# Sums over a head's 64 channels moved from TensorE products with ones to VectorE turns and GpSimd copies, in a FoX and RWKV-7 layer

## The chip, the cores and the metric

The kernel runs on one NeuronCore of a Trainium2 chip. The metric is device microseconds from start to end of one execution, as the median of several runs; lower is better.

## What is computed

The layer takes `x` of 256 frames by 4096 channels, all in float32. One projection `x @ w_in` gives the columns of 16 heads of forgetting attention (128 wide), of 32 heads of RWKV-7 time mixing (64 wide) and of a gate. The RWKV-7 part needs three sums over the 64 channels of a head, for each frame. In the reference they are:

```python
kk = (kr * k_k).reshape(hs)
kk = kk / jnp.maximum(jnp.linalg.norm(kk, axis=-1, keepdims=True), 1e-12)
...
y = _rwkv7_scan(rh, decay.reshape(hs), kh, vh, -kk, kk * ah)
mu = jnp.mean(y, axis=-1, keepdims=True)
var = jnp.mean(jnp.square(y - mu), axis=-1, keepdims=True)
y = ((y - mu) * lax.rsqrt(var + GN_EPS)).reshape(B, S, RWKV_WIDTH) * gn_gain + gn_bias
bonus = jnp.sum(rh * kh * r_k, axis=-1, keepdims=True) * vh
```

These are the squared norm of the key, the bonus sum of `r * k * r_k`, and the variance of the readout. Both head groups are then gated, multiplied by `w_out` (4096 x 4096), added to the scaled input and normalised.

## The kernel before

**The weight stream.** TensorE multiplies float32 data as two rounded halves: `split` (line 137) makes from a loaded tile `w` (128 x 1024) its high half `w_Nh` by ScalarE (line 140) and the low half `w_Nl` by VectorE (line 141). A product is then three matmuls of 128 x 512: x high by w high (line 146), x low by w high (147), x high by w low (148). A tile makes 12 such matmuls. The main loop goes over 8 pairs `n` of 128-channel groups, four blocks `b` per pair (r and k; v; two blocks of attention and gate columns) and 16 tiles a block; then the output projection (`project`, lines 849 to 854) goes over 8 column blocks in the same way. There are three buffers for low halves and four for high halves and for raw tiles.

**What runs beside it.** Everything else is written as Python generators (`ahead`, which runs `prepare` for the 16 groups, `chain`, which runs `rwkv` for the 8 pairs, `fox`, `unload`). The loop calls `slot()` after every two groups of three matmuls, and each call moves every generator on by one `yield`; `wait(W[...])` counts such slots. A scheduler below then sets the order on each engine's queue, and each queue runs in order. So VectorE's queue holds the weight splits with the pieces of all generators between them.

**`prepare(i)`, lines 451 to 503** (16 times). Two rows of 256 frames are made in `sb`: the squared key (ScalarE, line 470) and `r * r_k * k` (VectorE, 471). For their sums over the 64 partitions of a head, `sb` is split into halves `sh` (ScalarE, 475) and `sl` (VectorE, 476), and two matmuls with a 128 x 128 block matrix of ones (`onesr`, made at line 187 from the constants at 72 and 73) put the sums, already on all 64 partitions, into PSUM tile `nps` (490, 491). VectorE takes the maximum of the norm with 1e-24 (493) and its reciprocal over 256 columns (496); ScalarE copies the bonus sum into `bon` (494). The reciprocal goes into `ae` (498) and `BK` (501).

**`rwkv(n)`, lines 505 to 703** (8 times). After the chunked recurrence, the readout of a pair lies in PSUM tile `yp`. ScalarE squares it into `sd` (683) and copies it scaled (685); the squares are split (688, 689), two matmuls with `onesr` sum them into `vs` (692, 693), ScalarE takes the root of the 512 columns (694), and VectorE two reciprocals of 256 columns (696), two products (698) and two sums (699), ahead of the gate (`gate`, 371).

**GpSimd** is used for masks of the attention (`affine_select`, line 713, on a tile that SyncE's queue loads), for the token shift of v (521 to 523), for a product (519) and for zeroing `eL` (438) and `SV` (605); its queue runs in order too. The tile `shl` has one buffer, which is also used for `yr` and for `BKt` (546).

Of the kernel before, what the change touches and what calls it, by code (L numbers as in the profile page):

```python
# [10 lines left out]
F32 = mybir.dt.float32  # L11
BF16 = mybir.dt.bfloat16
F32R = mybir.dt.float32r
AF = mybir.ActivationFunctionType
ALU = mybir.AluOpType
AX = mybir.AxisListType

P = 128
S = 256
# [5 lines left out]
HD = 64  # L25
# [25 lines left out]
B = 32  # L51
# [1 line left out]
NJ = B // NG  # L53
C_ID = 0
C_MASK = 128
C_ONES = 256
C_E = 384
C_SCAN = 640
C_ROW = C_SCAN + S
C_W = C_ROW + 2  # L60
LW = 2 * LORA + NF


def constants():
    p = np.arange(P)[:, None]
    s = p % C
    t = np.arange(C)[None, :]
    cst = np.zeros((P, C_W), np.float32)
    cst[:, C_ID : C_ID + P] = np.eye(P)
    cst[:, C_MASK : C_MASK + C] = s < t  # L70
    cst[:, C_MASK + C : C_MASK + 2 * C] = s <= t
    same = (np.arange(P)[:, None] // HD) == (np.arange(P)[None, :] // HD)
    cst[:, C_ONES : C_ONES + P] = same
    j = (p % NG) * NJ + np.arange(P)[None, :] // B
    cst[:, C_E : C_E + P] = j == np.arange(P)[None, :] % B
    cst[:, C_SCAN : C_SCAN + S] = (np.arange(S)[None, :] % C) != 0
    first = np.array([1, 1, 0, 1, 0, 1], np.float32)
    sign = np.array([-1, -1, -1, 1, 1, 1], np.float32)
    cst[:6, C_ROW] = sign * (2 * first - 1)
    cst[:6, C_ROW + 1] = sign * (1 - first)  # L80
    return cst
# [3 lines left out]
def layer(ctx: ExitStack, tc: tile.TileContext, xt, xtok, w_lora, w_main, muv, w_o, up, par, mulora, fbias, lng, lnb, cst, out):  # L85
    nc = tc.nc
    PS = bass.MemoryType.PSUM

    const = ctx.enter_context(tc.tile_pool(name="const", bufs=1))
# [5 lines left out]
    def pst(name):  # L95
        return ps.tile([P, 512], F32, tag="ps", name=name)

    cs = const.tile([P, C_W], F32, name="cs")
# [14 lines left out]
    for n, (k0, k1) in enumerate(pieces):  # L113
        raw = spool.tile([P, 2 * S], F32, tag="xr", name=f"xr{n}", bufs=4)
        nc.sync.dma_start(out=raw[:, : (k1 - k0) * S], in_=xt[:, k0:k1, :].rearrange("p k t -> p (k t)"))
        x_raw.append(raw)
        raw = spool.tile([P, 2 * LW], F32, tag="lr", name=f"lr{n}", bufs=4)
        (nc.scalar if n < 3 else nc.sync).dma_start(out=raw[:, : (k1 - k0) * LW], in_=w_lora[:, k0:k1, :].rearrange("p k c -> p (k c)"))
        l_raw.append(raw)
# [9 lines left out]
    nc.sync.dma_start(out=cs, in_=cst)  # L129

    ident = cs[:, C_ID : C_ID + P]
    ones = cs[:, C_ONES : C_ONES + P]

    def column(name, i):
        return prm[:, PAR.index(name), i : i + 1]
# [21 lines left out]
    for n, (k0, k1) in enumerate(pieces):  # L157
        for k in range(k0, k1):
            t = xpool.tile([P, 2, S], F32R, tag=f"x{k}", name=f"x{k}")
            r = x_raw[n][:, (k - k0) * S : (k - k0 + 1) * S]  # L160
            tc.keep_in_program_order(nc.scalar.copy(t[:, 0, :], r))
            nc.vector.tensor_tensor(t[:, 1, :], r, t[:, 0, :].bitcast(F32), ALU.subtract)
            xs.append(t)
        hi, lo = split(l_raw[n], (k1 - k0) * LW, f"wl{n}", spool, str(n % 3), 2 * LW)
        for j, m in steps(k1 - k0, False):
            mm(acc_l[m], m, k0 + j, hi, lo, j * LW, LW)
        hi, lo = split(w_raw[n], (k1 - k0) * OB, f"wr{n}")
# [15 lines left out]
    nc.vector.tensor_scalar(hka[:, 1, :], prm[:, ika, :], -0.5, 1.0, ALU.mult, ALU.add)  # L183
    gneps = const.tile([P, 1], F32, name="gneps")
    nc.vector.memset(gneps, GN_EPS)
    onesr = const.tile([P, P], F32R, name="onesr")
    nc.vector.tensor_copy(onesr, ones)

    sides = []

# [70 lines left out]
    rp = mid.enter_context(tc.tile_pool(name="rp", bufs=1))  # L261
# [9 lines left out]
    def rt(name):  # L271
        return t256("t", name, 5)
# [122 lines left out]
    def flat(t):  # L395
        return t.rearrange("p a b -> p (a b)")
# [18 lines left out]
    def front(i):  # L415
# [19 lines left out]
        L = rt(f"L{i}")  # L435
        nc.vector.tensor_tensor_scan(L, cs[:, C_SCAN : C_SCAN + S], tw, 0.0, ALU.mult, ALU.add)
        eL = rp.tile([P, NCH, C + 1], F32, tag="eL", name=f"eL{i}")
# [10 lines left out]

    KB = [(slice(0, C), slice(C, P)), (slice(C, P), slice(0, C))]

    def prepare(i):
        n, u = divmod(i, 2)
        while u == 0 and n and n - 1 not in done:
            yield
        eL, eI, am, ae = yield from front(i)
        while (i, 1) not in rk:
            yield
        r, kr = rk[i, 0], rk[i, 1]
        if u == 0:
            pairs[n] = dict(  # L460
                lc=rp.tile([P, 2, NCH], F32, tag="lc", name=f"lc{n}"),
                BK=rp.tile([P, 2, NCH, P], F32, tag="BK", name=f"BK{n}"),
                lt=[rp.tile([P, 2, NCH, P], F32, tag=f"lt{j}", name=f"lt{j}_{n}") for j in range(2)],
                bon=rp.tile([P, 2, S], F32, tag="bon", name=f"bon{n}"),
            )
        q = pairs[n]
        k = rt(f"k{i}")
        nc.vector.tensor_tensor(k, kr, am, ALU.mult)
        sb = rp.tile([P, 2, S], F32, tag="Nb", name=f"sb{i}")
        nc.scalar.activation(sb[:, 0, :], kr, AF.Square, scale=column("k_k", i))  # L470
        nc.vector.scalar_tensor_tensor(sb[:, 1, :], r, column("r_k", i), k, ALU.mult, ALU.mult)
        yield
        shl = rp.tile([P, 2, 2, S], F32R, tag="shl", name=f"shl{i}")
        sh, sl = flat(shl[:, 0]), flat(shl[:, 1])
        nc.scalar.copy(sh, flat(sb))
        nc.vector.tensor_tensor(sl, flat(sb), sh.bitcast(F32), ALU.subtract)
        yield
        BK = q["BK"][:, u]
        lt = [q["lt"][j][:, u] for j in range(2)]
        nc.scalar.copy(q["lc"][:, u, :], eL[:, :, C])  # L480
        nc.vector.scalar_tensor_tensor(lt[0][:, :, 0:C], ch(kr), nkk[:, i : i + 1], eL[:, :, 0:C], ALU.mult, ALU.mult)
        nc.vector.tensor_tensor(lt[0][:, :, C:P], ch(r), eL[:, :, 1:], ALU.mult)
        nc.scalar.copy(lt[1][HALF[1]], lt[0][HALF[1]])
        yield
        for j in range(2):
            h = HALF[j]
            nc.vector.tensor_tensor(BK[h, :, KB[j][1]], ch(k)[h], ch(eI)[h], ALU.mult)
        yield from wait(W["np"] if n else 2 * W["np"])
        nps = pst(f"np{i}")
        nc.tensor.matmul(nps, onesr, sl, start=True, stop=False)  # L490
        nc.tensor.matmul(nps, onesr, sh, start=False, stop=True)
        n2 = rt(f"n2{i}")
        nc.vector.tensor_scalar(n2, nps[:, :S], 1e-24, None, ALU.max)
        nc.scalar.copy(q["bon"][:, u, :], nps[:, S:])
        yield
        tc.keep_in_program_order(nc.vector.reciprocal(n2, n2))
        yield from wait(2)
        nc.vector.scalar_tensor_tensor(ae, ae, 0.5, n2, ALU.mult, ALU.mult)
        for j in range(2):
            h = HALF[j]  # L500
            nc.vector.scalar_tensor_tensor(BK[h, :, KB[j][0]], ch(kr)[h], column("k_k", i)[h], ch(ae)[h], ALU.mult, ALU.mult)
        yield
        prepared.add(i)

    def rwkv(n):
# [3 lines left out]
        q = pairs[n]  # L509
        lc, BK, lt, bon = q["lc"], q["BK"], q["lt"], q["bon"]  # L510
# [9 lines left out]
        p, t = bks[n], vs_[n]  # L520
# [10 lines left out]
        for u in range(2):  # L531
# [3 lines left out]
            for a in range(4):  # L535
                o = B * (a % 2)
                nc.sync.dma_start(out=nd[u, a].rearrange("c r s -> r c s"), in_=gb[a // 2][B * a : B * (a + 1), u, :, o : o + B])
            nc.sync.dma_start(out=flat(nb[:, u]), in_=nd[u].rearrange("q c r s -> (q c) (r s)").unsqueeze(1).to_broadcast([16, NG, B * B]))
        for u in range(2):
            for j in range(2):  # L540
                o = HALF[1 - j]
# [30 lines left out]
        xc = rp.tile([P, 2, NJ, B], F32, tag="xc", name=f"xc{n}")  # L572
        ev = cs[:, C_E : C_E + P].rearrange("p (j s) -> p j s", s=B)
        for u in range(2):
# [21 lines left out]
        for j in range(2):  # L596
            o = HALF[1 - j]
# [9 lines left out]
        for a in range(4):  # L607
            o = C * (a // 2) + B * (a % 2)
# [3 lines left out]
        for u in range(2):  # L612
            for c in range(NCH):
                for j in range(2):
                    a, b = slice(C * j, C * j + B), slice(C * j + B, C * j + C)
# [17 lines left out]
        for u in range(2):  # L633
            for c in range(NCH):
                for j in range(2):
                    a, b = slice(C * j, C * j + B), slice(C * j + B, C * j + C)
                    nc.tensor.matmul(xp[a, u * P + c * B : u * P + (c + 1) * B], Q[b, u, c, :], X[b, u, c, C * j + B : C * j + C], start=True, stop=True)
        for j in range(2):
            a = slice(C * j, C * j + B)
# [7 lines left out]
        for c in range(NCH):  # L647
# [10 lines left out]
            if c < NCH - 1:  # L658
# [11 lines left out]
                if 0 < c + 1 < NCH - 1:  # L670
                    sl = rp.tile([P, 2, C], F32, tag="sl", name=f"sl{n}_{c}")
# [10 lines left out]
        yc, sd = post[:, 0:2], post[:, 2:4]  # L682
        nc.scalar.activation(flat(sd), yp, AF.Square)
        for u in range(2):
            nc.scalar.mul(yc[:, u], yp[:, u * S : (u + 1) * S], column("gn_gain", i0 + u))
        yr = rp.tile([P, 2, 2, S], F32R, tag="shl", name=f"yr{n}")
        yh, yl = flat(yr[:, 0]), flat(yr[:, 1])
        nc.scalar.copy(yh, flat(sd))
        nc.vector.tensor_tensor(yl, flat(sd), yh.bitcast(F32), ALU.subtract)
        yield from wait(W["vs"])  # L690
        vs = pst(f"vs{n}")
        nc.tensor.matmul(vs, onesr, yl, start=True, stop=False)
        nc.tensor.matmul(vs, onesr, yh, start=False, stop=True)
        nc.scalar.activation(flat(sd), vs, AF.Sqrt, scale=1.0 / HD, bias=gneps)
        for u in range(2):
            nc.vector.reciprocal(sd[:, u], sd[:, u])
            yield
            nc.vector.tensor_tensor(yc[:, u], yc[:, u], sd[:, u], ALU.mult)
            nc.vector.tensor_tensor(yc[:, u], yc[:, u], bon[:, u], ALU.add)
            while f"r{i0 + u}" not in szs or 2 * (i0 + u) + 1 >= FAR and not closed:  # L700
                yield
            yield from gate(yc[:, u], f"r{i0 + u}", 2 * (i0 + u) + 1)
# [208 lines left out]
    for b, q in outs:  # L911
        if q == 0:
            pool, tag = (ps, "ps") if b == 1 or b and b % 2 == 0 else (pp, "pp")
# [115 lines left out]
    for n in range(HALVED):  # L1029
        b = HALVED + n  # L1030
        finish(1, b, l1, pp, "pp")
        o = slice(n * OB, (n + 1) * OB)
# [52 lines left out]
```

## Time and profile before

| What | Value |
|---|---|
| Median of 3 runs | 1958.2 us (1957.36 to 1959.06) |
| Profiled execution, first to last instruction (span) | 1956.1 us |
| Profiled execution, time outside the span | not listed; the median run is 2.1 us above the span |
| TensorE busy | 1937.4 us, 99% of the span |
| VectorE busy | 1368.3 us, 70% |
| ScalarE busy | 981.2 us, 50% |
| GpSimd busy | 81.2 us, 4% |

Busy time is the time in which an engine has an instruction in work. Matmuls overlap one another: their records last longer than the distance from one to the next, and the cost of one is read from that distance. The page writes PE for TensorE, DVE for VectorE, ACT for ScalarE, POOL for GpSimd and SP for SyncE. L141 is line 141 of the kernel, and a name such as `w_7l` is the tile that the instruction writes.

### The profile page before, as it was taken

The numbers are of one execution on the slowest core, as the hardware profiler recorded it, in microseconds if no ns is written. First come the engines' busy times: TensorE is split into PE (matmuls) and PEld (weight loads), VectorE is DVE, ScalarE is ACT, GpSimd is POOL, SyncE is SP. The second block draws the span as 40 slices with busy tenths as digits, with TensorE's granted clock in tenths as the row PEclk, the third lists the DMA queues.
The fourth block names the chain that finished last, engine by engine and source line by source line (L and its number), as shares of the span: only waits on it lengthen the run. The fifth ranks groups of instructions, "written<-read, shape, count | busy, mean of one in ns | idle before, by whom it ended". The sixth has DMA issues, their size and how long they took to land.

```text
span 1956.1 us, 28202 instructions
## 1 busy us (share of the span) xinstructions
PE 1937.4 (99%) x10169; PEld 1586.9 (81%) x10169; DVE 1368.3 (70%) x2212; ACT 981.2 (50%) x1485; POOL 81.2 (4%) x111
## 2 busy tenths in 40 slices
PE   9998999999999999999999999999999999999998
PEld 7887778888887888788878887888788878888886
DVE  6587667866886688667857785778577856755555
ACT  6553555455545554565456545644564454433332
POOL 0010001000100010001000100010001000000000
PEclk9999999999999999999999999999999999999999
DMA  9577657867686778676867686778677777766564
GB/s 337 145 237 198 206 163 244 226 194 213 212 233 186 215 215 232 192 220 208 232 185 225 208 236 183 225 209 234 178 231 211 241 274 236 255 199 199 189 198 168
DMA packets 269392, 420.13 MB, mean 215 GB/s; under 512 B 142338, under 2 KB 171028, under 8 KB 269252
## 3 DMA queue, kind: packets, MB, share of 16 engines
q1 hardware_dynamic: 268820, 417.91, 70.7%
q8 instruction: 80, 1.31, 0.3%
q10 hardware_dynamic: 432, 0.43, 0.1%
q14 instruction: 60, 0.49, 0.1%
HBM read 388.61 MB, written 29.64 MB: 214 GB/s over the span
## 4 chain that ended last, share of the span: by engine, by line
PE 86%; DMA 1%; DVE 0%; ACT 0%; issue 0%; DVEq 0%; ACTq 0%; SPq 0%
PE acc L146 21%; PE acc L148 20%; PE acc L147 20%; PE oacc L852 6%; PE oacc L854 6%; PE oacc L853 6%; PE yp L678 1%; PE gp L517 1%; PE up L653 1%; PE rh L626 1%; PE sp L662 0%; DMA wo<-in_w_o_dram 0%; PE fsp L717 0%; PE fop L736 0%; PE tp L550 0%; DMA h<-hd 0%
## 5 line engine op out<-in xcount | busy, mean ns | idle before, releaser
L582 DVE TENSOR_REDUCE xc<-prod 128x8 f32<-128x16 f32 (+30 forms) x248 | 73.2, 295 | 6.7
L579 DVE TENSOR_TENSOR prod<-Nb,xc 128x8 f32<-128x8 f32 (+30 forms) x248 | 71.6, 289 | 6.6
L141 DVE TENSOR_TENSOR w_10l<-w,w_10h 128x1024 fp32r<-128x1024 f32 x31 | 37.9, 1223 | 37.8 <-PE acc L148 21.6
L141 DVE TENSOR_TENSOR w_6l<-w,w_6h 128x1024 fp32r<-128x1024 f32 x31 | 38.9, 1256 | 34.9 <-ACT w_6h L140 18.6
L141 DVE TENSOR_TENSOR w_8l<-w,w_8h 128x1024 fp32r<-128x1024 f32 x31 | 37.8, 1219 | 32.9 <-ACT UV L656 13.6
L141 DVE TENSOR_TENSOR w_0l<-w,w_0h 128x1024 fp32r<-128x1024 f32 x31 | 37.9, 1222 | 31.3 <-ACT w_0h L140 14.8
L141 DVE TENSOR_TENSOR w_5l<-w,w_5h 128x1024 fp32r<-128x1024 f32 x31 | 38.3, 1235 | 29.3 <-PE acc L148 17.4
L148 PE MATMUL acc<-w_7l,x 128*128 128x512 f32 x124 | 49.5, 399 | 5.4 <-DVE w_7l L141 5.4
L141 DVE TENSOR_TENSOR w_7l<-w,w_7h 128x1024 fp32r<-128x1024 f32 x31 | 37.9, 1222 | 22.3 <-PE acc L148 13.2
L141 DVE TENSOR_TENSOR w_11l<-w,w_11h 128x1024 fp32r<-128x1024 f32 x31 | 37.9, 1222 | 21.0 <-PE acc L148 13.5
L141 DVE TENSOR_TENSOR w_12l<-w,w_12h 128x1024 fp32r<-128x1024 f32 x31 | 37.5, 1211 | 20.6 <-PE acc L148 16.1
L141 DVE TENSOR_TENSOR w_14l<-w,w_14h 128x1024 fp32r<-128x1024 f32 x31 | 38.0, 1227 | 19.9 <-issue 11.1
L140 ACT CAST w_0h<-w 128x1024 fp32r<-128x1024 f32 x31 | 32.7, 1053 | 38.3 <-PE acc L147 21.7
L140 ACT CAST w_5h<-w 128x1024 fp32r<-128x1024 f32 x31 | 32.6, 1053 | 37.9 <-PE acc L147 37.9
L140 ACT CAST w_8h<-w 128x1024 fp32r<-128x1024 f32 x31 | 32.6, 1050 | 37.7 <-DMA w<-in_w_main_dram 31.3
L146 PE MATMUL acc<-w_7h,x 128*128 128x512 f32 x124 | 51.0, 411 | 0.0
L140 ACT CAST w_13h<-w 128x1024 fp32r<-128x1024 f32 x31 | 32.5, 1049 | 36.4 <-PE acc L147 22.9
L146 PE MATMUL acc<-w_5h,x 128*128 128x512 f32 x124 | 50.5, 408 | 0.0
L146 PE MATMUL acc<-w_8h,x 128*128 128x512 f32 x124 | 50.0, 404 | 0.4 <-ACT w_8h L140 0.4
L140 ACT CAST w_9h<-w 128x1024 fp32r<-128x1024 f32 x31 | 32.4, 1046 | 35.6 <-PE acc L147 32.9
L146 PE MATMUL acc<-w_3h,x 128*128 128x512 f32 x124 | 50.2, 405 | 0.0
L140 ACT CAST w_7h<-w 128x1024 fp32r<-128x1024 f32 x31 | 32.6, 1052 | 34.9 <-PE acc L147 19.7
(813 smaller groups left out, 6549.3 us busy)
## 6 DMA issues: line engine op xcount, KB each, us to landing
w<-in_w_main_dram SPq DMA_DIRECT2D x496, 512.0 KB, 3.9
wo<-in_w_o_dram SPq DMA_DIRECT2D x128, 512.0 KB, 3.8
bt<-bk SPq DMA_DIRECT2D x88, 128.0 KB, 4.0
Nb<-nd SPq DMA_DIRECT2D x16, 512.0 KB, 5.0
wr<-in_w_main_dram SPq DMA_DIRECT2D x15, 512.0 KB, 7.1
hd<-hl SPq DMA_DIRECT2D x29, 256.0 KB, 4.4
h<-hd SPq DMA_DIRECT2D x29, 256.0 KB, 6.1
raw<-bt SPq DMA_DIRECT2D x16, 256.0 KB
```

The costliest lines, as they stand in the source:

```text
L140: nc.scalar.copy(hi[:, :n], src[:, :n])
L141: nc.vector.tensor_tensor(lo[:, :n], src[:, :n], hi[:, :n].bitcast(F32), ALU.subtract)
L146: nc.tensor.matmul(acc[:, :n], xs[k][:, 0, tt], hi[:, o : o + n], start=(k == 0), stop=False)
L147: nc.tensor.matmul(acc[:, :n], xs[k][:, 1, tt], hi[:, o : o + n], start=False, stop=False)
L148: nc.tensor.matmul(acc[:, :n], xs[k][:, 0, tt], lo[:, o : o + n], start=False, stop=(k == KT - 1))
L517: nc.tensor.matmul(gp[u][j][:, c * P : (c + 1) * P], BK[h, u, c, :], lt[j][h, u, c, :], start=True, stop=True)
L579: first = nc.vector.tensor_tensor(prod[:, :, :, s + 1 :], nb[:, :, s : s + 1, s + 1 :].to_broadcast([P, 2, NJ, w]), xc[:, :, :, s + 1 :], ...
L582: nc.vector.tensor_reduce(xc[:, :, :, s : s + 1], prod[:, :, :, s:], AX.X, ALU.add)
L626: nc.tensor.matmul(rh[HALF[j], u * C : (u + 1) * C], lt[j][:, u, c, 0:C], SV[j][:, u, c, :], start=True, stop=True)
L852: nc.tensor.matmul(acc, ht[k][:, 0, tt], hi, start=(k == 0), stop=False)
L853: nc.tensor.matmul(acc, ht[k][:, 1, tt], hi, start=False, stop=False)
L854: nc.tensor.matmul(acc, ht[k][:, 0, tt], lo, start=False, stop=(k == KT - 1))
```

## The change

The sums over a head's 64 channels no longer use TensorE. `gather_heads` turns the 128 x 512 tile in 32 x 32 blocks, so that the 32 channels of a block lie side by side, and sums each run of 32 (16 columns remain). Four GpSimd copies bring to each quarter of 32 partitions the half sum of the other quarter of its head. VectorE adds the two. `spread` turns a column, read 32 times over, back onto all channels of the block. The maximum and the reciprocal in `prepare` work on 8 columns, the root and the reciprocal in `rwkv` on 16. The split halves, the matrix of ones and the two PSUM tiles go.

```diff
+QS = 2 * S // B
...
-    same = (np.arange(P)[:, None] // HD) == (np.arange(P)[None, :] // HD)
-    cst[:, C_ONES : C_ONES + P] = same
...
-    onesr = const.tile([P, P], F32R, name="onesr")
-    nc.vector.tensor_copy(onesr, ones)
...
+    def gather_heads(src, name):
+        t = rp.tile([P, 2 * S], F32, tag="shl", name=f"hq{name}")
+        nc.vector.transpose(t, src)
+        r = rp.tile([P, 2, QS], F32, tag="hr", name=f"hr{name}", bufs=2)
+        nc.vector.tensor_reduce(r[:, 0, :], t.rearrange("p (q f) -> p q f", f=B), AX.X, ALU.add)
+        for a in range(4):
+            o = a ^ 1
+            nc.gpsimd.tensor_copy(r[B * o : B * (o + 1), 1, :], r[B * a : B * (a + 1), 0, :])
+        return r
+
+    def spread(dst, val):
+        nc.vector.transpose(dst.rearrange("p (q f) -> p q f", f=B), val.unsqueeze(2).to_broadcast([P, val.shape[1], B]))
...
     def prepare(i):
...
-        shl = rp.tile([P, 2, 2, S], F32R, tag="shl", name=f"shl{i}")
-        sh, sl = flat(shl[:, 0]), flat(shl[:, 1])
-        nc.scalar.copy(sh, flat(sb))
-        nc.vector.tensor_tensor(sl, flat(sb), sh.bitcast(F32), ALU.subtract)
+        hr = gather_heads(flat(sb), i)
         yield
...
         yield from wait(W["np"] if n else 2 * W["np"])
-        nps = pst(f"np{i}")
-        nc.tensor.matmul(nps, onesr, sl, start=True, stop=False)
-        nc.tensor.matmul(nps, onesr, sh, start=False, stop=True)
-        n2 = rt(f"n2{i}")
-        nc.vector.tensor_scalar(n2, nps[:, :S], 1e-24, None, ALU.max)
-        nc.scalar.copy(q["bon"][:, u, :], nps[:, S:])
-        yield
-        tc.keep_in_program_order(nc.vector.reciprocal(n2, n2))
+        nc.vector.tensor_tensor(hr[:, 0, :], hr[:, 0, :], hr[:, 1, :], ALU.add)
+        n2 = hr[:, 1, : QS // 2]
+        nc.vector.tensor_scalar(n2, hr[:, 0, : QS // 2], 1e-24, None, ALU.max)
+        nc.vector.reciprocal(n2, n2)
+        yield
+        in2 = rt(f"n2{i}")
+        spread(in2, n2)
+        spread(q["bon"][:, u, :], hr[:, 0, QS // 2 :])
         yield from wait(2)
-        nc.vector.scalar_tensor_tensor(ae, ae, 0.5, n2, ALU.mult, ALU.mult)
+        nc.vector.scalar_tensor_tensor(ae, ae, 0.5, in2, ALU.mult, ALU.mult)
...
     def rwkv(n):
...
-        yr = rp.tile([P, 2, 2, S], F32R, tag="shl", name=f"yr{n}")
-        yh, yl = flat(yr[:, 0]), flat(yr[:, 1])
-        nc.scalar.copy(yh, flat(sd))
-        nc.vector.tensor_tensor(yl, flat(sd), yh.bitcast(F32), ALU.subtract)
+        hr = gather_heads(flat(sd), f"y{n}")
         yield from wait(W["vs"])
-        vs = pst(f"vs{n}")
-        nc.tensor.matmul(vs, onesr, yl, start=True, stop=False)
-        nc.tensor.matmul(vs, onesr, yh, start=False, stop=True)
-        nc.scalar.activation(flat(sd), vs, AF.Sqrt, scale=1.0 / HD, bias=gneps)
+        nc.vector.tensor_tensor(hr[:, 0, :], hr[:, 0, :], hr[:, 1, :], ALU.add)
+        nc.scalar.activation(hr[:, 0, :], hr[:, 0, :], AF.Sqrt, scale=1.0 / HD, bias=gneps)
+        nc.vector.reciprocal(hr[:, 1, :], hr[:, 0, :])
+        spread(flat(sd), hr[:, 1, :])
         for u in range(2):
-            nc.vector.reciprocal(sd[:, u], sd[:, u])
             yield
```

On the queues as the scheduler leaves them, TensorE has 48 matmuls fewer, ScalarE 40 instructions fewer, VectorE 79 more and GpSimd 96 copies more. In a steady pair, VectorE's queue after the change reads, in `rwkv`: turn, sum, split `w_10l`, the addition that waits for GpSimd, split `w_11l`, the reciprocal that waits for ScalarE, the spread; and in the second `prepare`: turn, product for `lt`, sum, split `w_0l`, two products for `BK`, split `w_1l`, the addition that waits for GpSimd, maximum, spread, reciprocal, spread. On GpSimd's queue the four copies of the first `prepare` stand behind the zeroing of `eL`, those of the second behind two masks and a zeroing of `eL`, those of `rwkv` behind the zeroing of the next `SV`.

More of the change, by code (lines that the diff above doesn't have):

```diff
@@ L55 @@
 C_MASK = 128
-C_ONES = 256
-C_E = 384
-C_SCAN = 640
+C_E = 256
+C_SCAN = 512
 C_ROW = C_SCAN + S
@@ L131, in layer @@
     ident = cs[:, C_ID : C_ID + P]
-    ones = cs[:, C_ONES : C_ONES + P]
     def column(name, i):
```

## Prediction

> **What bounds the kernel now.** I read the page's busy shares and chain first, then the list of TensorE's waits, then single instructions in order of time.
>
> ```profile
> span 1956.1 us, 28202 instructions
> ...
> PE 1937.4 (99%) x10169; PEld 1586.9 (81%) x10169; DVE 1368.3 (70%) x2212; ACT 981.2 (50%) x1485; POOL 81.2 (4%) x111
> ...
> PEclk9999999999999999999999999999999999999999
> ...
> PE 86%; DMA 1%; DVE 0%; ACT 0%; issue 0%; DVEq 0%; ACTq 0%; SPq 0%
> ```
>
> TensorE is busy for 99% of the span at its full granted clock, and the chain that ended last runs through TensorE alone (the shares that fall short of 100% are matmul records that the trace lacks). Busy time alone proves little for TensorE, so the list of whom it waited for decides:
>
> ```profile
> PE acc L148 <- DVE w_7l L141: 5.4, 1, 5.4
> PE zp L990 <- DVE zd L978: 1.4, 1, 1.4
> PE warmup L108 <- POOL idle L105: 1.3, 1, 1.3
> ...
> PE acc L148 <- DVE w_8l L141: 1.0, 1, 1.0
> ```
>
> These are the longest, with total, times and longest. They come to 9.1 us in 1956, each once, and all that follow are shorter. In a steady pair TensorE waits for nobody: a matmul is paid in full, and one taken away shortens the run by its own distance to the next, if the engines that feed TensorE keep up.
>
> **What is removed from TensorE.** Two matmuls of 128 x 512 in each of 16 `prepare` and two in each of 8 `rwkv`. The counts, and one pair in order of time with its successor:
>
> ```profile
> L490 PE MATMUL np<-shl,onesr x16: 388/388/388, 106.6 to 1486.0; 128*128 128x512 f32 x16
> L692 PE MATMUL vs<-yr,onesr x8: 388/388/388, 266.9 to 1614.2; 128*128 128x512 f32 x8
> ```
> ```profile
> 106.64 0.39 PE L490 MATMUL np<-shl,onesr 128*128 128x512 f32 x1
> 106.86 0.39 PE L491 MATMUL np<-shl,onesr 128*128 128x512 f32 x1
> 107.09 0.40 PE L146 MATMUL acc<-w_11h,x 128*128 128x512 f32 x1
> ```
>
> The 0.39 us overlap; the distance counts. From 106.64 to 107.09 are 0.45 us for the two, and the next matmul follows with no gap. So 24 pairs x 0.45 = **10.8 us** leave TensorE's queue.
>
> **What VectorE gets and loses.** It feeds TensorE with the low halves, in the same queue. Its rows (line, tile, count | busy us, mean ns | idle before):
>
> ```profile
> L476 DVE TENSOR_TENSOR shl<-sb,shl 128x512 fp32r<-128x512 f32 x16 | 10.9, 682 | 0.1
> L493 DVE TENSOR_SCALAR n<-np 128x256 f32<-128x256 f32 x16 | 6.8, 423 | 8.0 <-PE np L491 8.0
> L496 DVE RECIPROCAL n<-n 128x256 f32<-128x256 f32 x16 | 28.0, 1750 | 0.3
> L689 DVE TENSOR_TENSOR yr<-post,yr 128x512 fp32r<-128x512 f32 x8 | 5.5, 686 | 1.9 <-ACT yr L688 1.9
> L696 DVE RECIPROCAL post<-post 128x256 f32<-128x256 f32 x16 | 28.0, 1748 | 9.9 <-ACT post L694 9.9
> L781 DVE STREAM_TRANSPOSE bk<-bk 128x512 f32<-128x512 f32 x44 | 30.8, 702 | 4.6 <-ACT bk L890 4.4
> L594 DVE TENSOR_REDUCE vm<-vs 128x8 f32<-128x512 f32 x8 | 5.4, 669 | 0.0
> L558 DVE STREAM_TRANSPOSE UV<-vs 128x256 f32<-128x256 f32 x16 | 6.1, 420 | 0.0
> L725 DVE RECIPROCAL fst<-fst 128x1 f32<-128x1 f32 x32 | 4.9, 157 | 0.0
> ```
>
> The first five go, whole or with their columns cut; the last four are the nearest rows for what comes. A reciprocal costs 157 ns on 1 column and 1750 on 256, so (1750 - 157) / 255 = 6.2 ns a column: an estimated 200 ns on 8 columns and 250 on 16. The addition on 16 columns and the maximum on 8 have no row of their own; between the 157 ns of 1 column and the 423 of 256 I take 160 each, near the small end. The spread reads one column 32 times over, which no row does; I take it as any turn of its size, 420 or 702 ns.
>
> - `prepare`: out 682 + 423 + 1750 = 2855 ns; in 702 + 669 + 160 + 160 + 200 + 2 x 420 = 2731 ns. 0.12 us less, 16 times.
> - `rwkv`: out 686 + 2 x 1748 = 4182 ns; in 702 + 669 + 160 + 250 + 702 = 2483 ns. 1.70 us less, 8 times.
>
> VectorE thus loses 16 x 0.12 + 8 x 1.70 = 15.5 us. It is not what ends last, so this buys no time by itself; it is cover. With the small operations at 423 instead of 160 ns, `prepare` would gain 0.4 us, which the lead below covers.
>
> ScalarE loses a cast of 512 columns in both places and the copy of the bonus, and its root shrinks: no new load on any path.
>
> **How much lateness TensorE doesn't notice.** A low half is made ahead of its use. In the thinnest place of `rwkv`'s end, and in the thinnest around `prepare`, split and first use are:
>
> ```profile
> 460.70 1.23 DVE L141 TENSOR_TENSOR w_14l<-w,w_14h 128x1024 fp32r<-128x1024 f32 x1 [0.29 <-ACT w_14h L140]
> ...
> 520.59 1.16 DVE L141 TENSOR_TENSOR w_3l<-w,w_3h 128x1024 fp32r<-128x1024 f32 x1
> ```
> ```profile
> 464.22 0.39 PE L148 MATMUL acc<-w_14l,x 128*128 128x512 f32 x1
> ...
> 525.57 0.39 PE L148 MATMUL acc<-w_3l,x 128*128 128x512 f32 x1
> ```
>
> The leads are 464.22 - 461.93 = 2.29 us and 525.57 - 521.75 = 3.82 us. The first is thin because the two reciprocals (3.5 us) stand before it; they go, so about 2.29 + 1.70 = 3.99 us remain there.
>
> **The added wait.** VectorE's addition waits for four GpSimd copies of 32 x 16, and behind it in VectorE's queue stand the splits that TensorE needs. GpSimd's nearest rows:
>
> ```profile
> L438 POOL MEMSET eL<- 128x4 f32 x16 | 1.8, 111 | 346.1 <-DVE lt L481 338.0 <-DVE lt L482 8.0
> L605 POOL MEMSET SV<- 64x128 f32 x16 | 3.2, 200 | 199.9 <-PE yp L678 199.5
> L522 POOL TENSOR_TENSOR vs<-vs,muv 128x512 f32<-128x512 f32 x8 | 17.3, 2161 | 0.6
> ```
>
> A copy of 16 columns lies between 0.11 and 2.16 us (the longest mean of that engine that comes near); I take 0.15, near the 4 and 128 columns, so 0.6 us for four, with ends of 0.4 and 8.6. In `rwkv` a split of 1.2 us stands between the sum and the addition, in the second `prepare` two splits (2.4 us) and two products. So at my value the copies are done in time. The first `prepare` has even more between. GpSimd's queue adds no more: what stands before the copies waits for `lt` and `yp`, which VectorE and TensorE have finished before the sum, or for masks:
>
> ```profile
> 510.51 0.43 POOL L713 TENSOR_SCALAR_AFFINE_SELECT nb<-nb 128x128 f32<-128x128 f32 x1 [5.34 <-DMA nb<-ncd]
> 511.70 0.11 POOL L438 MEMSET eL<- 128x4 f32 x1 [0.76 <-DVE lt L482]
> ```
> ```profile
> 510.31 0.48 DVE L471 SCALAR_TENSOR_TENSOR sb<-s,prm,k 128x256 f32<-128x256 f32 x1
> ```
>
> The mask is over at 510.94, while `sb`, from which the turn starts, is only ready at 510.79, and turn and sum take 1.4 us more.
>
> One row speaks against the change: the same split takes 1.22 us, and 2.26, 1.04 more, when it starts just behind a GpSimd instruction.
>
> ```profile
> 131.14 1.29 POOL L521 TENSOR_TENSOR vs<-vs,bk 128x512 f32<-128x512 f32 x1 [10.53 <-DMA vs<-vd]
> ```
> ```profile
> 128.53 1.22 DVE L141 TENSOR_TENSOR w_5l<-w,w_5h 128x1024 fp32r<-128x1024 f32 x1 [1.49 <-PE acc L148]
> 131.25 2.26 DVE L141 TENSOR_TENSOR w_6l<-w,w_6h 128x1024 fp32r<-128x1024 f32 x1 [1.50 <-PE acc L148]
> ```
>
> So the two engines hold each other up. Then the copies may have to wait until the split behind the sum is over, and the 1.2 us of cover in `rwkv` are gone: the addition waits for the whole of the copies. At 0.6 us that is still far under the 3.99 us, and the sum stays; it is the point of the first rival that moves. The Trainium skill ("SBUF — State Buffer", section "SBUF: two separate sides") makes this a rule: a GpSimd instruction, or a VectorE instruction with two inputs in SBUF, takes a port pair that the two engines share whole, and the other blocks until it is done. By that rule the copies always wait for the split, without it they run beside it; the trace so far agrees with the rule, by the 1.04 us.
>
> **The sum.** 1956.1 - 10.8 = 1945.3 us for the span. The median of the runs is 2.1 us above the span, so **1947.4 us**, 0.55% less.
>
> **Rivals.**
>
> 1. *VectorE waits for GpSimd until TensorE starves (slower).* Place: the addition in `rwkv`. With no cover from the split, it decides from copies of 3.99 / 4 = 1.0 us each (with that cover from 1.3). At the upper end, 4 x 2.16 = 8.6 us, TensorE loses 8.6 - 4.0 = 4.6 us in each of 8 pairs, 37 us. A wait of that length also slows what follows:
>
> ```profile
> 192.27 0.79 PE L148 MATMUL acc<-w_7l,x 128*128 128x512 f32 x1 [5.37 <-DVE w_7l L141]
> 192.87 0.63 PE L146 MATMUL acc<-w_7h,x 128*128 128x512 f32 x1
> ...
> 195.43 0.45 PE L146 MATMUL acc<-w_7h,x 128*128 128x512 f32 x1
> ```
>
>    Six distances from 192.87 to 195.43 are 0.43 us each, not 0.225: 1.2 us more per wait, 10 us in 8. Together 1947.4 + 37 + 10 = 1994 us. Against it: GpSimd's small rows are 0.1 to 0.2 us, and 1.0 is five times that.
>
> 2. *No gain.* The time freed on TensorE is not had, because the weights arrive no faster, so 1958 us. For it: ScalarE does wait for weights.
>
> ```profile
> ACT w_8h L140 <- DMA w<-in_w_main_dram: 31.3, 12, 4.9
> ...
> q1 hardware_dynamic: 268820, 417.91, 70.7%
> ```
>
>    Against it: TensorE never waits for long after ScalarE, and the queue uses 70.7% of the engines' time; a stream 0.55% faster asks for 71.1%. Nor did the matmuls with ones stand in idle time: their neighbours follow without a gap.
>
> 3. *More gain.* The wait of 5.4 us in the first pair, the 1.0 behind it and the 1.2 of slow matmuls go too: 1947.4 - 7.6 = 1939.8 us. Against it: `w_7l` was late behind VectorE's own chain of products and sums, which stays in the same order.
>
> **How the numbers follow.** Forecast 83%, first rival 7%, second 6%, third 4%. A measurement can tell about 0.2% (3.9 us) from no change. Faster is forecast and third rival, 0.87; same is the second, 0.06; slower the first, 0.07. The forecast's own spread comes from the distance of the matmuls (0.22 to 0.23 us, so 10.6 to 11.0), the runs' own spread (1957.4 to 1959.1) and a few small waits, some 1945 to 1950. To take in some starving at copies just above 1.0 us, and a little of the third case, I give **1943.5 to 1952**.
>
> **What would show it.** Right: 48 matmuls fewer, TensorE's waits still a handful outside the steady pairs, VectorE busy near 1353 us, copies of 0.1 to 0.3 us, and VectorE's waits for `hr` under 1 us each. Wrong: rows of TensorE waiting for `w_...l` after an addition that GpSimd released; copies near 1 us or more; spreads far above 0.42 and 0.70 us; matmuls further apart than 0.23 us.

## The result, and the profile after

The changed kernel takes 1946.17 us (median of 4 runs, 1945.32 to 1946.65) against 1957.94 for the kernel before (4 runs, 1957.36 to 1959.06): a ratio of 0.9936, 95% interval 0.9924 to 0.9948, so 11.8 us less. The forecast was 1947.4. The profiled execution took 1945.32 us, the shortest of the four.

The page of the kernel after, the lines that answer to those of before:

```profile
span 1943.5 us, 28242 instructions
...
PE 1925.2 (99%) x10121; PEld 1578.9 (81%) x10121; DVE 1348.8 (69%) x2291; ACT 962.8 (50%) x1445; POOL 129.9 (7%) x207
...
PEclk9999999999999999999999999999999999999999
...
PE 96%; DVE 2%; DMA 0%; issue 0%; ACT 0%; SPq 0%; ACTq 0%; DVEq 0%
```

The picture is the same as before, only shorter: TensorE is busy for 99% of the span and ends last, with 48 matmuls fewer (10169 to 10121). TensorE lost 12.2 us of busy time and the span 12.6. VectorE lost 19.5 us (1368.3 to 1348.8). Whom TensorE waited for in the kernel after, with total, times and longest:

```profile
PE acc L145 <- DVE w_7l L138: 5.4, 1, 5.4
PE zp L991 <- DVE zd L979: 1.4, 1, 1.4
PE warmup L106 <- POOL idle L103: 1.3, 1, 1.3
PE acc L145 <- DVE w_10l L138: 1.3, 1, 1.3
PE acc L145 <- DVE w_8l L138: 1.0, 1, 1.0
```

Four of the five stood there before. New is `w_10l`, once, in the first pair; the wait of `xp` (1.1 us, once, in the kernel before: `PE xp L637 <- DVE Q L620: 1.1, 1, 1.1` in its list of waits) is gone. No steady pair has a wait.

The new operations in the kernel after (min/median/max ns, first and last start):

```profile
L453 POOL COPY hr<-hr x64: 194/376/3762, 103.5 to 1472.8; 32x16 f32<-32x16 f32 x64
L494 DVE TENSOR_TENSOR hr<-hr x16: 168/175/262, 109.0 to 1474.3; 128x16 f32<-128x16 f32 x16
L457 DVE STREAM_TRANSPOSE bon<-hr x16: 394/436/439, 109.7 to 1474.6; 128x256 f32<-128x256 f32 x16
L497 DVE RECIPROCAL hr<-hr x16: 152/158/196, 110.1 to 1475.0; 128x8 f32<-128x8 f32 x16
```
```profile
L453 POOL COPY hry<-hry x32: 186/192/1052, 266.2 to 1601.1; 32x16 f32<-32x16 f32 x32
L695 DVE RECIPROCAL hry<-hry x8: 243/244/248, 268.8 to 1602.5; 128x16 f32<-128x16 f32 x8
L457 DVE STREAM_TRANSPOSE post<-hry x8: 711/712/712, 269.1 to 1602.8; 128x512 f32<-128x512 f32 x8
```

VectorE's operations came out close to their estimates: 175 ns for the addition (160), 158 and 244 for the reciprocals (200 and 250), 436 and 712 for the spreads (420 and 702), so a column read 32 times over is turned at about the price of a plain tile. A copy takes 0.19 us when nothing holds it, but the median in `prepare` is 0.38 and the longest 3.8: it started at 105.02 and ended at 108.78, just behind three weight splits in a row on VectorE (105.24 to 108.73).

**Where the gain sits.** Matmuls in order of time, around one removed place (the second `prepare` of a pair), in the kernel before and after:

```profile
516.44 0.39 PE L146 MATMUL acc<-w_0h,x 128*128 128x512 f32 x1
...
517.57 0.40 PE L148 MATMUL acc<-w_0l,x 128*128 128x512 f32 x1
517.81 0.39 PE L490 MATMUL np<-shl,onesr 128*128 128x512 f32 x1
518.03 0.39 PE L491 MATMUL np<-shl,onesr 128*128 128x512 f32 x1
518.26 0.40 PE L146 MATMUL acc<-w_0h,x 128*128 128x512 f32 x1
...
520.35 0.39 PE L146 MATMUL acc<-w_1h,x 128*128 128x512 f32 x1
```
```profile
513.82 0.39 PE L143 MATMUL acc<-w_0h,x 128*128 128x512 f32 x1
...
516.54 0.39 PE L143 MATMUL acc<-w_1h,x 128*128 128x512 f32 x1
...
517.22 0.39 PE L143 MATMUL acc<-w_1h,x 128*128 128x512 f32 x1
```

From the first matmul of the block to the sixteenth of the weight stream are 520.35 - 516.44 = 3.91 us before and 517.22 - 513.82 = 3.40 after: 0.51 us for one place. The undisturbed distance is 2.72 / 12 = 0.227 us (513.82 to 516.54), so two matmuls by themselves are 0.45; the other 0.06 us are in the neighbours of the pair, which stood 0.23 to 0.24 apart. The other places are like this one: in the kernel before, the two matmuls take 0.45 or 0.46 us in all 24, and the ten behind them 2.31 or 2.32 us in 23, where ten undisturbed ones take 2.27 (in the last place, matmuls of the attention follow). 24 places x 0.51 = 12.2 us. The rest is small: 1.3 lost at `w_10l`, 1.1 gained at `xp`, which leaves about 0.6 net for other short gaps, together the 12.6 us of the span.

### The profile page after: what moved, and what is told of

It reads as the page before. It is cut to its first block, busy times and chain, and to the rows that moved or that the text cites. A ratio compares the mean times of both kernels' runs of the same rounds, so it can differ in the third digit from the quotient of the medians.

```text
span 1943.5 us, 28242 instructions
## 1 busy us (share of the span) xinstructions
PE 1925.2 (99%) x10121; PEld 1578.9 (81%) x10121; DVE 1348.8 (69%) x2291; ACT 962.8 (50%) x1445; POOL 129.9 (7%) x207
## 4 chain that ended last, share of the span: by engine, by line
PE 96%; DVE 2%; DMA 0%; issue 0%; ACT 0%; SPq 0%; ACTq 0%; DVEq 0%
PE acc L143 24%; PE acc L145 23%; PE acc L144 23%; PE oacc L853 6%; PE oacc L855 6%; PE oacc L854 6%; PE yp L683 1%; PE gp L522 1%; PE up L658 1%; PE rh L631 1%; PE sp L667 0%; DVE prod L584 0%; DVE xc L587 0%; PE tp L555 0%; PE fsp L718 0%
## 5 line engine op out<-in xcount | busy, mean ns | idle before, releaser
L714 POOL TENSOR_SCALAR_AFFINE_SELECT nb<-nb 128x128 f32<-128x128 f32 x32 | 14.5, 455 | 727.5 <-DMA nb<-ncd 284.0
L137 ACT CAST w_15h<-w 128x1024 fp32r<-128x1024 f32 x31 | 32.7, 1054 | 36.9 <-PE acc L144 27.2
L143 PE MATMUL acc<-w_6h,x 128*128 128x512 f32 x124 | 49.9, 402 | 0.0
L137 ACT CAST w_10h<-w 128x1024 fp32r<-128x1024 f32 x31 | 32.5, 1049 | 35.0 <-PE acc L144 30.9
L143 PE MATMUL acc<-w_2h,x 128*128 128x512 f32 x124 | 49.6, 400 | 0.0
```

Of the source, the lines that this page charges most:

```text
L137: nc.scalar.copy(hi[:, :n], src[:, :n])
L143: nc.tensor.matmul(acc[:, :n], xs[k][:, 0, tt], hi[:, o : o + n], start=(k == 0), stop=False)
```

## The experiments

**1. Two matmuls put back, and four.** To the kernel after come matmuls with a tile of ones that nobody reads, two or four for each of the 24 places; VectorE keeps its new work. They sum over 96 partitions (96x512 in the trace), not over 128 as in the kernel before, and not 128 x 512 as the expectations say.

```diff
+    def products(name):
+        t = pst(name)
+        for j in range(2):
+            nc.tensor.matmul(t, oner, flat(lr[:, j % 2]), start=(j == 0), stop=(j == 1))
...
         yield from wait(W["np"] if n else 2 * W["np"])
+        products(f"np{i}")
...
         yield from wait(W["vs"])
+        products(f"vp{n}")
```

> The changed kernel with 48 matmuls of 128 x 512 put back on TensorE, two in each prepare and two in each rwkv, whose results nobody reads. VectorE, ScalarE and GpSimd keep the changed work. If the gain is TensorE's time, it goes back by what two matmuls and their place cost in the trace of before, 24 x 0.51 = 12.3 us: 1946.2 + 12.3 = 1958.5 us, the time of the kernel before. If the gain came from VectorE's lighter queue, the time stays near 1946 us.

> As the run with products put back, but four matmuls at each place, 96 in all, again read by nobody. The trace of before shows 0.51 us for two and their place where two distances are 0.45 us. If the 0.06 us belong to the place (a disturbed run of matmuls), the cost is 24 x (4 x 0.227 + 0.06) = 23.2 us: 1969.4 us. If each such matmul costs 0.257 us, it is 24.7 us: 1970.9 us. If VectorE set the gain: still 1946 us.

With two: 1957.24 us, ratio to the kernel before 0.9999 (0.9989 to 1.0008), span 1954.5. With four: 1967.76 us, ratio 1.0051 (1.0034 to 1.0068), span 1965.9. So the whole gain goes when TensorE gets two matmuls back, though VectorE stays at 1353.6 us and ScalarE at 961.9: the gain is TensorE's time. The first 48 cost 11.0 us of span, the next 48 11.4; by the medians it is 11.5 and 10.5, so 0.22 to 0.24 us each, and four a place came out under both numbers expected. That is near their own distance, below the 0.51 a place of the removal. The scheduler put many of these matmuls, which hang on nothing, elsewhere, beside other short groups. But eight pairs do stand between two groups of three as the removed ones did, and the ten matmuls behind them take 2.28 or 2.29 us, 0.02 over undisturbed ones and not 0.05. Experiment 7 takes that up.

**2. Short reciprocals in the kernel before.** The other candidate for the gain is VectorE's relief.

```diff
-        tc.keep_in_program_order(nc.vector.reciprocal(n2, n2))
+        tc.keep_in_program_order(nc.vector.tensor_scalar(n2, n2, 2.5e-10, None, ALU.mult))
...
-            nc.vector.reciprocal(sd[:, u], sd[:, u])
+            nc.vector.tensor_scalar(sd[:, u], sd[:, u], 0.01, None, ALU.mult)
```

> The kernel before, with the matmuls with ones, but each of its 32 reciprocals over 256 columns is replaced by a product with a constant, so the values are not the reference's. VectorE gets about 32 x (1.75 - 0.29) = 47 us less, three times what the change takes from it. If TensorE's time sets the end: no change, 1957.9 us within 0.2%. If a lighter VectorE queue gives the gain: faster by at least the 12 us of the change, 1946 us or less.

1957.53 us, ratio 1.0 (0.999 to 1.0009). The page of this kernel shows how much VectorE lost:

```profile
PE 1937.6 (99%) x10169; PEld 1589.5 (81%) x10169; DVE 1333.9 (68%) x2212; ACT 981.9 (50%) x1485; POOL 87.4 (4%) x111
```

34.4 us of VectorE's busy time gone (1368.3 to 1333.9), and nothing gained. It is less than the 47 us expected, though the 32 operations themselves went from 56.0 us to 9.2: the splits `w_5l` and `w_6l` took 7.6 us more, and the rest was not followed up. It is still more than twice the 15.5 us that the change was to take from VectorE. VectorE's relief is cover and nothing else.

**3. One half of the change alone.** The norm and the bonus in `prepare` changed and `rwkv` as before, and the reverse (the edits are those of the change itself).

> Only the part in prepare is changed (norm and bonus), the variance keeps its matmuls. If the gain is TensorE's time it is that of 16 places, 16 x 0.51 = 8.2 us, less the 1.3 us that TensorE waits for w_10l in the first pair after the change: 1957.9 - 6.9 = 1951.0 us (1949.7 if that wait is not due to this part). If VectorE's lighter queue gave the gain, this part, which takes only 0.12 us each from VectorE, gives almost nothing: 1957 us.

> Only the part in rwkv is changed (variance), norm and bonus keep their matmuls. TensorE's time: 8 places x 0.51 = 4.1 us, 1953.8 us. VectorE's lighter queue: nearly the whole gain, since 8 x 1.70 = 13.6 of the 15.5 us that VectorE loses lie here: about 1947 us.

`prepare` alone: 1951.39 us, ratio 0.9966 (0.9955 to 0.9978). `rwkv` alone: 1954.05, ratio 0.9982 (0.9972 to 0.9991). Against 1958.33 for the kernel before, run beside them, these are 6.9 us for 16 places and 4.3 for 8, 11.2 together, close to the 11.8 of the whole. Both are the numbers of TensorE's time (1951.0 and 1953.8 expected), and neither is that of VectorE's lighter queue (1957 and 1947). `prepare` gives less per place (0.43) than `rwkv` (0.54), because the new wait for `w_10l` (1.2 us here, none with `rwkv` alone) comes with `prepare`; without it 8.1 / 16 = 0.51.

**4. The first pair's order.** This takes up the third rival: the waits for `w_7l` and those around it. In the first pair, the later rows of VectorE's own chain of products and sums (in `rwkv`) are issued after the last split but one, where the scheduler had put them ahead of `w_7l`.

```diff
+        lows.append(low.ins)
...
+            if n == 0 and t > 8:
+                with tc.issue_after(lows[-2]):
+                    first = row(s, w, prod, nb, xc)
+            else:
+                first = row(s, w, prod, nb, xc)
```

> The changed kernel, and in the first pair the rows of VectorE's chain of products and sums are each issued only after the last split but one, so that the chain does not stand in one piece ahead of a split. If the wait of 5.4 us of TensorE there, the 1.0 us behind it and the slow matmuls after it (1.2 us) are all due to that order, they go: 1946.2 - 7.6 = 1938.6 us. If the chain only ends later and something else waits for it, the time stays near 1946 us or grows.

1937.62 us, ratio to the kernel before 0.9896 (0.9881 to 0.9911). That is 19.8 us under the kernel before run beside it, where the change as it stands was 11.8 under: about 8 us more, and the fastest version here. TensorE's longest waits in it:

```profile
PE zp L1001 <- DVE zd L989: 1.4, 1, 1.4
PE warmup L106 <- POOL idle L103: 1.3, 1, 1.3
PE acc L148 <- DVE w_10l L140: 1.3, 1, 1.3
PE acc L148 <- DVE w_8l L140: 1.0, 1, 1.0
```

The 5.4 us are gone; the span falls by 7.7 us, more than the wait, as the slow matmuls behind it go as well (in the kernel after nine distances of 0.43 us). The wait for `w_8l` stays, so it was no consequence of the one before it, though the third rival counted it as one.

**5. Four and eight times as many copies.** Each copy on GpSimd is made four or eight times over, 16 or 32 in a row. This finds the point from which the added wait decides.

```diff
-        for a in range(4):
+        for a in [a for _ in range(4) for a in range(4)]:
```

> The changed kernel with each set of four GpSimd copies made four times over, 16 copies in place of 4. The trace after shows 0.19 us for a copy that nothing holds up, so 12 x 0.19 = 2.3 us more wait at each addition; in rwkv VectorE then waits 0.8 + 2.3 = 3.1 us. If TensorE's lead of about 4 us covers it, the time stays at 1946 us within 0.2%. If any wait of VectorE reaches TensorE, 8 x 2.3 = 18 us or more: 1964 us.

> 32 copies in place of 4 at each sum: 28 x 0.19 = 5.3 us more. In rwkv VectorE waits 0.8 + 5.3 = 6.1 us, 2.1 us over the lead of 4.0 us, 17 us in 8 pairs; in the second prepare about 5 us over a lead of 2.5, 21 us; with slow matmuls after such waits some 5 to 10 us more. That is the first rival of the prediction made to happen: about 1985 us (1965 to 2010). If GpSimd's copies run beside everything: 1946 us.

Four times: 1952.85 us, ratio 0.9973 (0.9961 to 0.9984), 6.7 us over the change. Neither theory's number. Where VectorE waited, and where one block starts in the second pair and in the last (kernel after: 321.73, and 1521.24):

```profile
DVE hr L494 <- POOL hr L453: 45.9, 16, 3.3
...
DVE hry L693 <- POOL hry L453: 30.0, 8, 4.1
```
```profile
328.38 0.39 PE L143 MATMUL acc<-w_0h,x 128*128 128x512 f32 x1
...
1528.83 0.39 PE L143 MATMUL acc<-w_0h,x 128*128 128x512 f32 x1
```

At the second pair this kernel is 6.65 us behind, at the last one 7.59. So nearly the whole loss is made in the first pairs, where a late `w_2l` costs 2.6 us of waiting and eight slow matmuls behind it, and TensorE waits once for the attention, 1.2 us. In the steady pairs VectorE waits 2.9 and 3.8 us in every place and TensorE loses 0.9 us in 1200. There, the theory that the lead covers holds; it failed for the start, where there is no lead.

Eight times: 2051.6 us, ratio 1.0479 (1.0463 to 1.0494), 105 us over the change and far over what either theory gave. VectorE's waits and TensorE's:

```profile
DVE hr L494 <- POOL hr L453: 109.1, 16, 7.3
DVE hry L693 <- POOL hry L453: 60.4, 8, 7.8
```
```profile
PE acc L145 <- DVE w_2l L138: 45.9, 8, 6.1
PE acc L145 <- DVE w_11l L138: 13.1, 6, 2.2
```

The first rival's mechanism is thus real, but its main place is not the end of `rwkv` (`w_11l`, 2.2 us each) that I named; it is the second `prepare`, whose next split is `w_2l`. One such wait on TensorE's queue, in order of time:

```profile
353.65 0.79 PE L145 MATMUL acc<-w_2l,x 128*128 128x512 f32 x1 [5.68 <-DVE w_2l L138]
354.25 0.63 PE L143 MATMUL acc<-w_2h,x 128*128 128x512 f32 x1
...
356.38 0.59 PE L145 MATMUL acc<-w_2l,x 128*128 128x512 f32 x1
```

Behind the wait the matmuls come 0.43 us apart (five distances from 354.25 to 356.38), at about half pace, and in the other seven places of this kind for seven to eleven distances. Of the six waits of 2.2 us for `w_11l`, three are followed by such slow matmuls and three are not. One of each:

```profile
892.53 0.69 PE L145 MATMUL acc<-w_11l,x 128*128 128x512 f32 x1 [2.18 <-DVE w_11l L138]
893.01 0.63 PE L143 MATMUL acc<-w_11h,x 128*128 128x512 f32 x1
...
895.57 0.63 PE L143 MATMUL acc<-w_11h,x 128*128 128x512 f32 x1
```
```profile
483.92 0.50 PE L145 MATMUL acc<-w_11l,x 128*128 128x512 f32 x1 [2.18 <-DVE w_11l L138]
484.25 0.39 PE L143 MATMUL acc<-w_11h,x 128*128 128x512 f32 x1
...
486.10 0.39 PE L145 MATMUL acc<-w_11l,x 128*128 128x512 f32 x1
```

Six distances of 0.43 us in the first, eight of 0.23 in the second. The granted clock is 0.53 from 892.5 to 895.5 and 1.00 from 483.9 to 486.9. The Trainium skill ("TensorE: Matmul & The Clock Gate", Part 1) says that the array's clock is halved after an idle window of some 3.4 us, and gives 426.7 ns between matmuls of 512 columns in that state. The trace agrees with the pace, 0.43 us, but not with 3.4 us as the least wait: here 2.2 us were enough in three of six places, and 2.6 us in the run with four times as many copies. What decides between the three and the three was not found. TensorE's waits in this run come to 83 us, 72 more than in the kernel after; the other 33 of the 105 us are such slow matmuls and waits too short to list, and were not split further.

**6. The copies on VectorE.**

```diff
-            nc.gpsimd.tensor_copy(r[B * o : B * (o + 1), 1, :], r[B * a : B * (a + 1), 0, :])
+            nc.vector.tensor_copy(r[B * o : B * (o + 1), 1, :], r[B * a : B * (a + 1), 0, :])
```

> The changed kernel with the four copies of each place on VectorE in place of GpSimd (96 copies; everything is computed). Price by the nearest row, VectorE's 128x16 addition of 0.175 us: four come to 0.6 to 0.7 us, 24 places to 14 to 17 us more in VectorE's queue, nothing waited for. Theory (TensorE bounds, leads of 1.5 us and more in the steady pairs cover): 1946 us, the same as the change within 0.1%, VectorE busy about 1364. Rival (the port that the two engines share costs the GpSimd form something on the path): 1 to 2 us less than the change. Second rival (VectorE's queue is the thinner place: w_0l and w_1l have leads of only 1.5 to 2.3 us near the end of rwkv): a few tenths lost in each of 8 pairs, 1948 us.

1946.58 us, ratio 0.9942 (0.9925 to 0.9958), span 1943.6: the change's own time. The page's busy shares and the copies:

```profile
PE 1925.3 (99%) x10121; PEld 1579.1 (81%) x10121; DVE 1363.1 (70%) x2387; ACT 963.5 (50%) x1445; POOL 77.7 (4%) x111
```
```profile
L453 DVE COPY hr<-hr x64: 161/166/171, 104.5 to 1473.4; 32x16 f32<-32x16 f32 x64
```

A copy takes 0.166 us and is held by nothing; VectorE carries 14.3 us more and the time stays (TensorE has one new wait, of 0.3 us for `w_11l` in the first pair). GpSimd is not what makes the change work, and the two engines' holding each other up costs nothing here.

**7. The products unread.** Open was the 0.06 us a place that the two matmuls themselves don't explain. In the kernel before, the 48 products stay, in the same order on TensorE's queue, and nobody reads them.

```diff
-        nc.vector.tensor_scalar(n2, nps[:, :S], 1e-24, None, ALU.max)
-        nc.scalar.copy(q["bon"][:, u, :], nps[:, S:])
+        nc.vector.tensor_scalar(n2, sb[:, 0, :], 6.0e4, None, ALU.max)
+        nc.scalar.copy(q["bon"][:, u, :], sb[:, 1, :])
...
-        nc.scalar.activation(flat(sd), vs, AF.Sqrt, scale=1.0 / HD, bias=gneps)
+        nc.scalar.activation(flat(sd), flat(sd), AF.Sqrt, scale=1.0 / HD, bias=gneps)
```

> The kernel before, with its 48 matmuls with ones in their old places on TensorE's queue (the queue is the same, instruction for instruction), but nobody reads what they put into PSUM: the maximum and the copy of the bonus read sb, the root reads sd. The sums over a head are left out, so norms, bonus and variance are not the reference's. The question: each removed place gave 0.51 to 0.52 us where the two matmuls' own distances are 0.45; in the trace of before the ten matmuls behind a pair come to 0.05 us more than ten undisturbed ones. Theory P (TensorE's own: whatever stands between two groups of three slows what follows): the ten matmuls behind a pair stay 0.05 us over, time 1957 to 1958 us, at most the 1.1 us of the xp wait less. Theory R (VectorE and ScalarE reading those PSUM tiles, or the waits hung on them, slow the matmuls that run meanwhile): they come even at 0.227 each, 24 x 0.05 = 1.2 us are gained, span about 1954.9. The trace's distances tell them apart, not the time.

1957.03 us, ratio 0.9996 (0.9985 to 1.0006), span 1954.5. The same stretch as above, in this kernel:

```profile
516.43 0.39 PE L146 MATMUL acc<-w_0h,x 128*128 128x512 f32 x1
...
520.35 0.39 PE L146 MATMUL acc<-w_1h,x 128*128 128x512 f32 x1
```

3.92 us, as before (3.91), not the 3.85 of 17 undisturbed distances; and the ten matmuls behind a pair take 2.31 or 2.32 us in 23 of 24 places, as before. So the 0.06 us hang neither on the readers of those PSUM tiles nor on the waits for them; theory R falls. Theory P as it was put, that whatever stands between two groups slows what follows, isn't shown either: in experiment 1 eight pairs stand so and cost only 0.02. Those pairs differ in their operands (96 partitions, other tiles), and VectorE's work beside them differs too. Which of these makes the neighbours slower was not found.

## Why the prediction was right, point by point

- **The bound** was right: two matmuls put back on TensorE take the whole gain (experiment 1), and 34 us less work on VectorE brings none (2). My list of TensorE's longest waits passed over one, `xp` with 1.1 us; with it they come to 10.2 us and not 9.1, which changes nothing in the argument.
- **The removal** was right in kind and mis-sized: 24 x 0.45 = 10.8 us were forecast and 24 x 0.51 = 12.2 measured. I read the pair's own distance and took the next matmul's start as the end of the matter. The ten matmuls behind it still bore 0.05 us. These 1.4 us, with 0.4 us net of small waits, are the 1.8 us by which the profiled span came out lower (1943.5, not 1945.3). The time came out 1.2 lower; a difference so small is within the runs' spread, and it is the distances in the traces that show the step.
- **VectorE's books** were right: with the measured durations, `prepare` loses 2855 - 2743 = 112 ns and `rwkv` 4182 - 2528 = 1654, so 16 x 0.11 + 8 x 1.65 = 15.0 us (15.5 forecast). The page's busy time fell by 19.5; 3.1 of the other 4.5 us are a single cast near the end, `identr`, that the change doesn't touch and that took 3.28 us before and 0.23 after.
- **The added wait** was covered, as forecast, but not because copies are fast. I took 0.6 us for four; in `rwkv` they took 1.74, as the sentence on the two engines holding each other up had allowed. The kernel after, VectorE's queue and GpSimd's:

```profile
445.32 0.69 DVE L450 TENSOR_REDUCE hry<-hqy 128x16 f32<-128x512 f32 x1
445.92 1.22 DVE L138 TENSOR_TENSOR w_10l<-w,w_10h 128x1024 fp32r<-128x1024 f32 x1
447.92 0.18 DVE L693 TENSOR_TENSOR hry<-hry 128x16 f32<-128x16 f32 x1 [0.78 <-POOL hry L453]
```
```profile
446.14 1.74 POOL L453 COPY hry<-hry 32x16 f32<-32x16 f32 x4 [1.70 <-DVE hry L450]
```

  The first copy took 1.05 us (the longest of `hry` above) and so ended at 447.19, just as the split ended (447.14); the other three took 0.19 each, and VectorE waited 0.78 us, under the 1 us forecast. The Trainium skill's rule ("SBUF — State Buffer", section "SBUF: two separate sides"), that a VectorE instruction with two SBUF inputs and a GpSimd instruction that reads SBUF don't run side by side, fits that; the rival reading, that the split hides the copies, does not. In the second `prepare` it is the same: the four took 3.08 us, from 510.75 to 513.83, and ended just behind the second of the two splits (513.77), so VectorE hardly waited there. My sign of being right, copies of 0.1 to 0.3 us, thus failed in `prepare`, and my sign of being wrong, copies near 1 us, came true without harm: a copy that is held until the split ends costs VectorE only the copies behind it.
- **The leads.** They grew where I said (`w_14l` in `rwkv` has 4.40 us, from 2.29). Around the second `prepare` they shrank, which I hadn't looked for: `w_0l` there has 2.52 us, from 4.21. And the thinnest place near the new work is now at the block behind `rwkv`, which I hadn't listed:

```profile
466.23 1.22 DVE L138 TENSOR_TENSOR w_0l<-w,w_0h 128x1024 fp32r<-128x1024 f32 x1
```
```profile
468.95 0.39 PE L145 MATMUL acc<-w_0l,x 128*128 128x512 f32 x1
```

  468.95 - 467.45 = 1.50 us. It sufficed, but the cover is smaller than my 3.99. (`w_7l`, away from the new work, has only 0.77 us in this pair, before and after.)
- **The first rival** is the right mechanism with the wrong place and price. In the steady pairs 16 copies (VectorE waits 2.9 and 3.8 us) are still covered and 32 are not, which brackets my 3.99 us; the first pairs starve earlier, and the price at 32 copies, with VectorE's waits of 6.8 and 7.6 us, is 105 us and not the 47 that I gave for 8.6, because `prepare`, with its shrunken leads, starves as well, and half pace follows its waits.
- **The second rival** fell: in the kernel after, TensorE's longest wait for ScalarE is 0.2 us. **The third** did not come by itself; made on purpose, it gives about 8 us (experiment 4), and my 7.6 was near, in part by luck: it counted 1.0 us for `w_8l`, which stays, and 1.2 us of slow matmuls, which were 1.8 in the kernel after.
- **Missed**: the wait for `w_10l` in the first pair. The turn and the sum are issued ahead of the split there, which starts at 103.31 and not at 102.04, 1.27 us later, and TensorE was already there:

```profile
103.31 1.21 DVE L138 TENSOR_TENSOR w_10l<-w,w_10h 128x1024 fp32r<-128x1024 f32 x1
```
```profile
104.58 0.73 PE L145 MATMUL acc<-w_10l,x 128*128 128x512 f32 x2 [1.25 <-DVE w_10l L138]
```

## What to carry to other kernels

On an engine that never waits, work taken off is paid back at the distance between its instructions, and here a little more, as it interrupted a regular stream; look at ten neighbours, not at the gap alone. Price the relief of an engine that doesn't end last at nothing, but look for every place where its queue has little lead, the start of the run above all: there, a microsecond put ahead of a split is paid in full.

## What the runs showed of the hardware that was not expected

- The pair of matmuls with ones over 128 partitions, put between groups of three, slowed the matmuls around it by about 0.06 us in sum (0.23 to 0.24 us apart, not 0.227), whether its result was read or not. A pair over 96 partitions, in eight places of the same kind, slowed the ten behind it by 0.02.
- Waits of TensorE of 2.2 us were followed by matmuls at half pace (0.43 us apart) in three of six places.
- A copy of 32 x 16 from one quarter of the partitions to another takes 0.19 us on GpSimd when nothing holds it, but up to 3.8 us beside VectorE's splits, and 0.166 us on VectorE.
- A turn whose input is one column read 32 times over takes about as long as any turn of its output (436 and 712 ns, where rows of that size took 420 and 702).
